# Operands of all projections at set distances in SBUF, with fewer places for staged copies

## The chip, the core and the metric

The kernel runs on one core of a Trainium2 chip. The core has a matrix engine (TensorE, PE in the profile, with its weight loads shown apart as PEld), a vector engine (DVE), a scalar engine (ACT), a general engine (POOL) and a sync engine (SP), which here only issues DMA transfers. All five run their own instruction streams and meet at semaphores. The metric is the device time of one execution in microseconds; the time before is 1488.55 us, the median of 3 runs (1488.12 to 1489.94).

## What is computed

One inference step of a one-layer streaming encoder: 1024 new frames (prompt) and 64 frames of a running stream (sample), 1088 tokens of 1024 features in all. Cut to what matters:

```python
def mixer(xn, conv_prefix, attn_fn, w_in, w_conv, w_conv_out, w_attn_out, w_out):
    proj = xn @ w_in
    cb, cc, ch, q, k, v, ga, gb = jnp.split(proj, splits, axis=-1)
    cv, conv_state = causal_conv(cc * ch, conv_prefix, w_conv)
    ya = (cb * cv) @ w_conv_out
    o, new_k, new_v = attn_fn(heads(q), heads(k), heads(v))
    yb = o.reshape(B, L, ATT_DIM) @ w_attn_out
    merged = jax.nn.sigmoid(ga) * ya + jax.nn.sigmoid(gb) * yb
    return merged @ w_out, conv_state, new_k, new_v

def swiglu(x, w1, w3, w2):
    return (jax.nn.silu(x @ w1) * (x @ w3)) @ w2

x = x + mixer(rmsnorm(x, g_mix), ...)
x = x + swiglu(rmsnorm(x, g_ffn), w_ff1, w_ff3, w_ff2)
return rmsnorm(x, g_final), ...
```

attn_fn is attention over the own chunk of 64 frames and the 8 before it, and q, k, v are 512 wide, ga and gb 1024, the inner size of swiglu is 2816. All is float32; the new key, value and convolution states are returned too.

## The kernel before

A float32 product is made of three products of a reduced type (F32R): `split` (L126, L127) writes the high part of an operand and the rest, called l = 0 and l = 1 for x and `hi` and `lo` (tags `wh`, `wl`) for weights, and hi times l0, hi times l1 and lo times l0 are summed in PSUM. The matrices of the input projection and of both parts of swiglu are moreover multiplied in halves with seven products of sums of blocks in place of eight (`STEPS`); the sums of x's blocks are tiles of their own (xs, tt), made once, and xn and mg are the plain blocks. All projections have features on the output's partitions and tokens in the columns: HT = 544 is half of the tokens, HN = 272 a quarter, and a matmul with 272 columns takes one quarter.

L246 in `run` is the inner statement of the seven-product projections: for each of four k it issues three matmuls (`hi` l0, `hi` l1, `lo` l0) on each of two quarters. Its x lies in [128, 2, 4, 544] tiles, that is l, then k, then the tokens, so that the two parts of one k are four rows apart; its weights lie in [128, 4, 128] tiles, a step of k after the other. L308 to L310 in `product` are the three terms of a plain product on quarters (the gates ga and gb, and the output projections of convolution and attention, whose operands u and ob are [128, 2, 4, 1088]). L487 to L489 in the v projection and L1101 to L1103 in w_out's projection have tokens on the partitions and 512 columns of weights moving. L1579 is the down projection of swiglu, which reads the inner values back from HBM (`ht`) as weights and 512 columns of w_ff2 from the rings `ring`; L1421 is the same for the 64 sample frames.

The stages in time, read from the trace by line: v projection and norm to 66 us, input units (q, k, cc, ch, cb, part of gb) to 328, gates with the attention between them to 560, merge to 678, w_out to 782, up projections of swiglu to 1252, then the down projection. Copies are staged on the way: `scr` is one region of SBUF in which `slot` hands out places by turns (`SNAP` for copies of partial sums out of PSUM, `CC` for the products cc, ch and k, `V32` for v rows on their way to the returned cache, `STAGE`, `UT` and so on), and a writer of a place waits until its last reader, often a DMA, is done. `st_pool` holds the gates on their way to HBM (`gst`), from which `gates_in` reads them back in the merge. Generators in the text (`ahead`, `prep`) mix the making of the next unit's weights into the running one, and that sets the order on the computing engines. On SP the order of the loads follows their destinations too: a load stands behind the work that frees its tile, and may stand far ahead of the place where the text asks for it. SP stops at a load whose destination is not yet free, and with it all loads behind. The first load of w2r (`early`, tag raw) is such a one.

## Time and profile before

| | |
|---|---|
| median of 3 runs | 1488.55 us |
| profiled execution | 1488.62 us |
| its span | 1486.9 us |
| mean granted clock of TensorE | 0.999 |
| stage of the up projections, busy time of PE in 462.00 us | 460.28 us, 3643 matmuls |
| stage of the down projection, in 235.00 us | 226.33 us, 1008 matmuls |
| input units, in 262.00 us | 261.44 us, 2080 matmuls |

The span is the time from the first to the last instruction in the profile; the execution's time lies 1.7 us above it. A matmul's busy time in the trace is that of one instruction from start to modelled end, and neighbours overlap; the interval between the starts of neighbours is what adds up to the stage. In the chain of waits a row like "PE Db L246 x24" gives when a group of 24 such matmuls began and how long it took until the next.

### The profile page before, as it was taken

To read this page: it belongs to the slowest core of one execution; us is meant where nothing else is said; L and a number is where in the kernel's file an instruction comes from. 1 tells how busy PE (TensorE), PEld (TensorE's weight loads), DVE (VectorE), ACT (ScalarE), POOL (GpSimd) and SP (SyncE) were. 2 spreads that over 40 slices of the span, in tenths; PEclk is the share of its full clock that TensorE was granted. 3 is DMA by queue.
4 is the path that set the end of the run, shared out by engine and by line. 5 is a ranking of instruction groups with operands and counts; after the bars stand their busy time and mean duration, and the time that the engine had idled before them with its cause. 6 is when DMAs were issued, how large, how long until landed. Compare 5 with 4: busy or idle time off the path is not lost.

```text
span 1486.9 us, 26478 instructions
## 1 busy us (share of the span) xinstructions
PE 1471.3 (99%) x10200; PEld 1380.9 (93%) x10200; DVE 982.5 (66%) x1852; ACT 681.7 (46%) x1398; POOL 129.9 (9%) x238
## 2 busy tenths in 40 slices
PE   9999999999999999999999999999999999999997
PEld 6899999999989999998889999999999999888886
DVE  7975565633777754763489667666666668857676
ACT  7654333434776653631356444444444445412223
POOL 1300010001111121000100111110011111000000
PEclk9999999999999999999999999999999999999999
DMA  8686623177776539645432454443344438767675
GB/s 290 183 275 209 202 66 113 58 219 222 191 190 180 146 109 297 194 122 174 150 106 79 146 184 156 160 146 117 114 146 154 152 149 306 262 227 238 224 265 202
DMA packets 166494, 264.73 MB, mean 178 GB/s; under 512 B 18912, under 2 KB 103072, under 8 KB 166208
## 3 DMA queue, kind: packets, MB, share of 16 engines
q1 hardware_dynamic: 145584, 196.13, 42.4%
q0 software_dynamic: 19632, 64.81, 12.1%
q10 hardware_dynamic: 1152, 2.10, 0.4%
q8 instruction: 80, 1.31, 0.4%
q14 instruction: 46, 0.38, 0.1%
HBM read 172.89 MB, written 91.92 MB: 178 GB/s over the span
## 4 chain that ended last, share of the span: by engine, by line
PE 95%; DVE 3%; DMA 1%; ACT 1%; issue 0%; SPq 0%; ACTq 0%; DVEq 0%
PE Ab L246 9%; PE Aa L246 9%; PE A L1579 8%; PE Db L246 4%; PE Da L246 4%; PE D L1579 4%; PE g L309 3%; PE g L308 3%; PE g L310 3%; PE Bb L246 2%; PE Ba L246 2%; PE B L1579 2%; PE wo L1102 2%; PE wo L1101 2%; PE wo L1103 2%; PE t L927 2%
## 5 line engine op out<-in xcount | busy, mean ns | idle before, releaser
L1579 PE MATMUL A<-ring,ht 128*128 128x512 f32 x528 | 124.3, 389 | 0.0
L1579 PEld LDWEIGHTS A<-ring,ht 128*128 128x128 f32 x528 | 98.9, 188 | 21.1 <-ACT acc L1589 0.6
L308 PE MATMUL g<-xn,whp 128*128 128x272 f32 x384 | 112.8, 294 | 0.0
L309 PE MATMUL g<-xn,whp 128*128 128x272 f32 x384 | 111.8, 291 | 0.0
L310 PE MATMUL g<-xn,wlp 128*128 128x272 f32 x384 | 111.1, 289 | 0.0
L126 ACT CAST ring<-w2r 128x512 fp32r<-128x512 f32 (+1 forms) x78 | 42.6, 587 | 89.5 <-PE A L1579 50.0
L126 ACT CAST hq<-sa 128x512 fp32r<-128x512 f32 x73 | 45.2, 619 | 80.5 <-DVE sa L1293 56.8
L838 DVE CUSTOM_DVE_ANT_0 p<-s,bb 128x640 f32<-128x640 f32 (+5 forms) x72 | 47.6, 662 | 42.4 <-PE s L881 40.6
L1277 POOL DMA_DIRECT2D h_d<-hq x73 | 38.9, 533 | 406.8 <-DVE hq L127 217.4
L308 PEld LDWEIGHTS g<-xn,whp 128*128 128x128 f32 x384 | 72.3, 188 | 0.9
L310 PEld LDWEIGHTS g<-xn,wlp 128*128 128x128 f32 x384 | 72.3, 188 | 0.5
L309 PEld LDWEIGHTS g<-xn,whp 128*128 128x128 f32 x384 | 72.4, 189 | 0.3
L127 DVE TENSOR_TENSOR hq<-sa,hq 128x512 fp32r<-128x512 f32 x73 | 50.4, 690 | 28.5 <-ACT hq L126 28.3
L127 DVE TENSOR_TENSOR wla<-rawa,wha 128x512 fp32r<-128x512 f32 x56 | 38.4, 688 | 39.6 <-ACT wha L126 39.6
L1579 PE MATMUL D<-ring,ht 128*128 128x512 f32 x264 | 62.6, 389 | 0.0
L246 PE MATMUL Aa<-tt,wha 128*128 128x272 f32 x352 | 58.4, 288 | 0.8 <-ACT sa_Q L234 0.8
L1579 PEld LDWEIGHTS D<-ring,ht 128*128 128x128 f32 x264 | 49.6, 188 | 10.3
L246 PE MATMUL Aa<-mg,wha 128*128 128x272 f32 x352 | 58.4, 288 | 0.4 <-DVE sa L1258 0.4
L246 PE MATMUL Ab<-mg,whb 128*128 128x272 f32 x352 | 58.6, 288 | 0.0
L246 PE MATMUL Ab<-tt,whb 128*128 128x272 f32 x352 | 58.4, 288 | 0.0
L126 ACT CAST wha<-rawa 128x512 fp32r<-128x512 f32 x56 | 34.6, 620 | 51.3 <-PE Ab L246 35.0
L127 DVE TENSOR_TENSOR ring<-w2r,ring 128x512 fp32r<-128x512 f32 (+1 forms) x78 | 48.7, 646 | 11.4 <-ACT ring L126 11.3
(531 smaller groups left out, 4379.8 us busy)
## 6 DMA issues: line engine op xcount, KB each, us to landing
ht<-h_d SPq DMA_DIRECT2D x154, 256.0 KB, 3.5
h_d<-hq POOLq DMA_DIRECT2D x73, 512.0 KB, 3.5
w2r<-in_w_ff SPq DMA_DIRECT2D x11, 1024.0 KB, 5.8
rawa<-in_w_ff SPq DMA_DIRECT2D x11, 1024.0 KB, 5.7
rawb<-in_w_ff SPq DMA_DIRECT2D x11, 1024.0 KB, 5.4
qd<-q_d SPq DMA_DIRECT2D x32, 272.0 KB, 4.7
rawp<-in_w_in SPq DMA_DIRECT2D x6, 1024.0 KB, 6.3
u_d<-scr SPq DMA_DIRECT2D x8, 544.0 KB, 5.2
```

What stands on the lines that cost most here:

```text
L126: a = act.copy(hi, src)
L127: b = vec.tensor_tensor(lo, src, hi.bitcast(F32), op=ALU.subtract)
L246: newest[0] = mm(t[:, j, :HN], w[:, k, :], x[p][:, l, k, j * HN : (j + 1) * HN], start=p in (1, 2, 7) and k == 0 and n == 0, stop=k == 3 a ...
L308: mm(out, a, p, start=k == 0, stop=False)
L309: mm(out, a, q, start=False, stop=False)
L310: mm(out, b, p, start=False, stop=k == kt - 1)
L838: vec.tensor_tensor_reduce(out=s if len(ps.shape) == 2 else s.rearrange("p (a b) -> p a b", a=2), in0=ps, in1=bias if len(ps.shape) == 2 e ...
L927: nc.tensor.transpose(tp[:, i * P : (i + 1) * P], s[:, i * P : (i + 1) * P], ident)
L1101: mm(ps, x(k, 0), wh, start=f, stop=False)
L1102: mm(ps, x(k, 0), wl, start=False, stop=False)
L1277: stored[0] = nc.gpsimd.dma_start(h_d[p, c - 1], hq.rearrange("p i l t -> p (i l t)").bitcast(F32)).ins
L1579: mm(t, ht[k][:, j, x], w[:, l], start=p in (1, 2, 7) and k == 0 and n == 0, stop=k == len(ks) - 1 and n == 2, skip_group_check=p in (6, 5 ...
```

## The change

It alters where operands lie, and gives other things fewer places.

- x's tiles (xn, mg, xs, tt; `operand`) become [k][l][tokens], the two parts of one k side by side, with rows of ROW = 552 floats of which the first 8 are unused; a lead of 8 floats stands ahead of xs.
- Weights (`pair`) get a step of 144 floats from k to k instead of 128, the high part beginning 8 floats into its tile. Where weights move (`moving_pair`: v and w_out) the high part of k begins at (56 + 16k) mod 64 floats and the low part at 16k mod 64. w_conv_out's and w_attn_out's weights get offsets of their own (`shift`) at the old step.
- u and ob get 8 floats between their two parts. In `product` the first two of the three terms change places for xn's even quarters.
- Staged copies: SNAP 4 places (5 before), CC 2 (3), a list KF for k's halves, V32 1 (2), `st_pool` 4 (5); gb is read back in 8 loads of [128, 1088] instead of 32 of [128, 272]; hs is one tile of two halves; two of the sums in the frames' norm lie in a `two_sums` tile of `early`; an accumulator moves from `dp` to `hp`; two of the four groups of cache transposes (`cache_tile`) come one step later.

```diff
 LAST = 3
+ROW, STEP = HT + 8, 144
 WARM = (14, 8)
...
         h = o // HT
-        return self.t[k // 4, h][:, l, k % 4, o - h * HT : o - h * HT + n]
+        return self.t[k // 4, h][:, k % 4, l, o - h * HT : o - h * HT + n]
...
+    def operand(pool, p, nm):
+        t = pool.tile([P, 8 * ROW], F32R, tag=f"o{p}", name=nm)
+        return t.rearrange("p (k l n) -> p k l n", k=4, l=2)[:, :, :, 8:]
+
+    def slots(nm):
+        return [ws.tile([P, 4 * STEP], F32R, tag=t, name=t + nm) for t in ("wh", "wl")]
+
+    def pair(nm):
+        hi, lo = (t.rearrange("p (k n) -> p k n", k=4) for t in slots(nm))
+        return hi[:, :, 8 : 8 + P], lo[:, :, :P]
+
+    def moved(nm, a, b):
+        hi, lo = slots(nm)
+        return hi[:, a : a + 512], lo[:, b : b + 512]
+
+    def moving_pair(nm, k):
+        return moved(nm, (56 + 16 * k) % 64, 16 * k % 64)
+
     def quarters(nm):
         return Quarters(
-            {gh: apool.tile([P, 2, 4, HT], F32R, tag=f"o{p}", name=f"{nm}{gh[0]}{gh[1]}") for p, gh in PLAIN.items()}
+            {gh: operand(apool, p, f"{nm}{gh[0]}{gh[1]}") for p, gh in PLAIN.items()}
         )
 
     def three_sums(pool, nm):
-        return {p: pool.tile([P, 2, 4, HT], F32R, tag=f"o{p}", name=f"{nm}{p}") for p in (6, 7, 5)}
+        return {p: operand(pool, p, f"{nm}{p}") for p in (6, 7, 5)}
 
     def both(t, c, n, src):
-        return split(t[:, 0, :, c : c + n], t[:, 1, :, c : c + n], src)
+        return split(t[:, :, 0, c : c + n], t[:, :, 1, c : c + n], src)
...
         def plain(self, p, src):
-            self.w[p] = [
-                ws.tile([P, 4, P], F32R, tag=t, name=f"{t}{self.nm}_{p}") for t in ("wh", "wl")
-            ]
+            self.w[p] = pair(f"{self.nm}_{p}")
             self.cast = split(*self.w[p], src)[0]
...
                         newest[0] = mm(
-                            t[:, j, :HN], w[:, k, :], x[p][:, l, k, j * HN : (j + 1) * HN],
+                            t[:, j, :HN], w[:, k, :], x[p][:, k, l, j * HN : (j + 1) * HN],
                             start=p in (1, 2, 7) and k == 0 and n == 0,
...
             for k in range(0, kt, 4):
-                hi, lo = (ws.tile([P, 4, P], F32R, tag=t, name=f"{t}p{prep.n}_{k}") for t in ("wh", "wl"))
+                nm = f"p{prep.n}_{k}"
+                if "shift" in ld:
+                    hi, lo = (t.rearrange("p (k n) -> p k n", k=4) for t in moved(nm, *ld["shift"]))
+                else:
+                    hi, lo = pair(nm)
                 split(hi, lo, ld["raw"][:, k : k + 4, at : at + P])
...
             p, q = x.at(0, k, o, n), x.at(1, k, o, n)
-            mm(out, a, p, start=k == 0, stop=False)
-            mm(out, a, q, start=False, stop=False)
+            first, then = (q, p) if x is xn and o // HN % 2 == 0 else (p, q)
+            mm(out, a, first, start=k == 0, stop=False)
+            mm(out, a, then, start=False, stop=False)
             mm(out, b, p, start=False, stop=k == kt - 1)
...
     for m in range(0, 8, 2):
-        lds = [{"src": ins[nm][0][:, m * P : (m + 2) * P], "w": 2 * P} for nm in ("w_conv_out", "w_attn_out")]
+        lds = [
+            {"src": ins[nm][0][:, m * P : (m + 2) * P], "w": 2 * P, "shift": shift}
+            for nm, shift in (("w_conv_out", (56, 24)), ("w_attn_out", (8, 40)))
+        ]
         plan += [(ld, 4, j * P) for ld in lds for j in range(2)]
...
     t1_pool = t1_stack.enter_context(tc.tile_pool(name="t1_pool", bufs=1, reuse_waits="tile"))
+    t1_pool.tile([P, 8], F32, name="lead1")
     t1 = three_sums(t1_pool, "xs")
 
-    scr = t1_pool.tile([P, 11496], F32, name="scr")
-    X, GM, SUMS, KEPT, VST, SQ, FEW = (0, 1024, 9312), 2048, 3072, (4096, 5120), (6144, 7168), 8192, 9264
-    V32 = [10336, 10848]
-    SNAP, STAGE, CC, UT = [544 * i for i in range(5)], [2720, 3808, 9312], [4896, 5988, 10400], [7080, 8172]
-    turn = {tuple(CC): 1}
+    scr = t1_pool.tile([P, 10816], F32, name="scr")
+    X, GM, SUMS, KEPT, VST, SQ, FEW = (0, 1024, 9264), 2048, 3072, (4096, 5120), (6144, 7168), 8192, 9216
+    V32 = [10288]
+    SNAP, STAGE, CC, UT = [544 * i for i in range(4)], [2720, 3808, 9264], [4896, 5988], [7080, 8172]
+    KF = [*CC, 2176]
+    turn = {tuple(KF): 0}
...
         for k in range(4):
-            hi, lo = (ws.tile([P, 512], F32R, tag=t, name=f"{t}v{half}_{k}") for t in ("wh", "wl"))
+            hi, lo = moving_pair(f"v{half}_{k}", k)
             if behind is None:
...
             x21_d[:, :, c : c + n],
-            xn.t[0, 1][:, :, :, c : c + n].rearrange("p l k t -> p (l k) t").bitcast(F32),
+            xn.t[0, 1][:, :, :, c : c + n].rearrange("p k l t -> p (k l) t").bitcast(F32),
         )
...
         def f(r, h, src, snap):
-            kf = slot(CC, HT)
+            kf = slot(KF, HT)
             whole(kf, src, snap)
...
         for _ in r:
-            if n < 2 and si in (2, 5):
+            if n < 2 and si in (2 + n, 5 + n):
                 i = 2 * n + si // 5
...
     pmm = pg_stack.enter_context(tc.tile_pool(name="pmm", bufs=3, space=PSUM, reuse_waits="tile"))
-    st_pool = pg_stack.enter_context(tc.tile_pool(name="st_pool", bufs=5, reuse_waits="tile"))
+    st_pool = pg_stack.enter_context(tc.tile_pool(name="st_pool", bufs=4, reuse_waits="tile"))
     att_stack = ExitStack()
...
     def gates_in(nm, m):
+        if nm == "gb":
+            t = mp.tile([P, T], F32, tag="rc", name=f"gb{m}", bufs=3)
+            nc.sync.dma_start(t, gb_d[m * P : (m + 1) * P])
+            for o, n in PIECES:
+                sg[nm, m, o] = t[:, o : o + n]
+            return
         for o, n in PIECES:
-            t = sg[nm, m, o] = mp.tile([P, HN], F32, tag=nm, name=f"{nm}{m}_{o}", bufs=8 if nm == "ga" else 4)
-            nc.sync.dma_start(t, (ga_d if nm == "ga" else gb_d)[m * P : (m + 1) * P, o : o + n])
+            t = sg[nm, m, o] = mp.tile([P, HN], F32, tag=nm, name=f"{nm}{m}_{o}", bufs=8)
+            nc.sync.dma_start(t, ga_d[m * P : (m + 1) * P, o : o + n])
 
     head_load(0)
 
-    nc.sync.dma_start(xn.t[0, 1].rearrange("p l k t -> p (l k) t").bitcast(F32), x21_d)
+    nc.sync.dma_start(xn.t[0, 1].rearrange("p k l t -> p (k l) t").bitcast(F32), x21_d)
     for i in range(4):
...
             uo = pg_stack.enter_context(tc.tile_pool(name="uo", bufs=1, reuse_waits="tile"))
-            u = Acts(uo.tile([P, 2, 4, T], F32R, name="u"))
-            ob = Acts(uo.tile([P, 2, 4, T], F32R, name="ob"))
+            u, ob = (
+                Acts(
+                    uo.tile([P, 2, 4 * T + 8], F32R, name=nm)[:, :, : 4 * T].rearrange("p l (k t) -> p l k t", k=4)
+                )
+                for nm in ("u", "ob")
+            )
             mp = pg_stack.enter_context(tc.tile_pool(name="mgp", bufs=4, reuse_waits="tile"))
...
             for k in range(4):
-                hi = ws.tile([P, 512], F32R, tag="wh", name=f"woh{hf}_{kq}_{k}")
-                lo = ws.tile([P, 512], F32R, tag="wl", name=f"wol{hf}_{kq}_{k}")
+                hi, lo = moving_pair(f"o{hf}_{kq}_{k}", k)
                 split(hi, lo, raw[:, k])
...
+        two_sums = early.tile([P, 2, D], F32, tag="raw", name="two_sums")
         w = wo_half(0)
...
             f = left.pop(c)
-            tag = "x1" if c == 384 else "sums"
-            s = wp.tile([P, D], F32, tag=tag, name=f"sums{c}", bufs=2 if c == 384 else 1)
+            if c == 384:
+                s = wp.tile([P, D], F32, tag="x1", name="sums384")
+            else:
+                s = two_sums[:, ORDER.index(8 if c == 512 else c // P + 4) // 2 % 2]
             s = s.rearrange("p (a k t) -> p a k t", a=2, k=4)[:, :, :, :n]
...
     LATE = {7: 1, 5: 2, 6: 6, 3: 7}
-    stored, last_keep, kept_now = [None], [], []
+    stored, last_keep, kept_now, both_hs = [None], [], [], {}
     names = [(l, p) for p in range(NF // 2) for l in "ab"]
...
                 return
-            hs = hp.tile([P, 2, 2, TS], F32R, tag="hs", name=f"hs{p}")
+            if "hs" not in both_hs:
+                both_hs["hs"] = hp.tile([P, 2, 256], F32R, tag="hs", name="hs", bufs=1)
+            hs = both_hs["hs"][:, p % 2].rearrange("p (r l t) -> p r l t", r=2, l=2)
             a, b, c, d = g[0, 0], g[0, 1], g[1, 0], g[1, 1]
...
             pool = apool if p in (1, 2, 4, 3) else tpool
-            ring[p] = pool.tile([P, 8 * HT], F32R, tag=f"o{p}", name=f"ring{p}")
+            ring[p] = pool.tile([P, 8 * ROW], F32R, tag=f"o{p}", name=f"ring{p}")[:, : 8 * HT]
         return ring[p]
...
         for kp in ks:
-            t = ws.tile([P, 2, 2, P], F32R, tag=("wh", "wl")[loaded[0] % 2], name=f"ht{kp}_{g}_{p}")
+            t = ws.tile([P, 4 * STEP], F32R, tag=("wh", "wl")[loaded[0] % 2], name=f"ht{kp}_{g}_{p}")
+            t = t[:, :512].rearrange("p (i l t) -> p i l t", i=2, l=2)
             loaded[0] += 1
...
     order = [(i + 4 * h, d) for g in range(2) for h, d in ((0, 0), (1, 0), (1, 1), (0, 1)) for i in (2 * g, 2 * g + 1)]
-    homes = [(dp, "acc")] + [(hp, "snap")] * 3 + [(hp, "sa"), (hp0, "snap"), (hp0, "sa")] + [(hp, "sa")] * 3
-    bufs = {(dp, "acc"): 1, (hp, "snap"): 3, (hp, "sa"): 4, (hp0, "snap"): 1, (hp0, "sa"): 1}
+    homes = [(hp, "snap")] * 3 + [(hp0, "snap"), (hp0, "sa")] + [(hp, "sa")] * 4 + [(hp, "hs")]
+    bufs = {(hp, "hs"): 1, (hp, "snap"): 3, (hp, "sa"): 4, (hp0, "snap"): 1, (hp0, "sa"): 1}
     for n, (i, d) in enumerate(order):```

Where the order of instructions moves. On TensorE, in the second unit of q (`Aq` and `Dq` are its sums in PSUM, xs and xn the moving x, `whq` and `wlq` its weights of step 6, 7 and so on; `ckp` are transposes of the key cache), before:

```order
L246 MATMUL Aq_788<-xs_103,whq_6_912 128x272 x4
L246 MATMUL Aq_788<-xs_103,wlq_6_913 128x272 x2
L701 MATMUL ckp_1094<-ident,scr 128x128 x4
L246 MATMUL Dq_1117<-xs_104,whq_7_943 128x272 x4
L246 MATMUL Dq_1117<-xs_104,wlq_7_944 128x272 x2
```

and in the changed kernel:

```order
L263 MATMUL Dq_1106<-xs_105,whq_7_944 128x272 x4
L263 MATMUL Dq_1106<-xs_105,wlq_7_945 128x272 x2
L728 MATMUL ckp_1135<-ident,scr 128x128 x4
L263 MATMUL Aq_789<-xs_106,whq_5_977 128x272 x4
L263 MATMUL Aq_789<-xs_106,wlq_5_978 128x272 x2
```

The third group of cache transposes stands behind step 7 instead of step 6, the fourth likewise one step later; nothing else on TensorE changes its place, and each k still issues four matmuls on the high part and two on the low one.

On SP, at the end of the merge (`gb` and `ga` are the gates read back, `w2r` a part of w_ff2, `xr` and `x_` residual rows, `wor` parts of w_out), before:

```order
L989 DMA gb_0_8161<-gb_d 128x272
L989 DMA gb_272_8163<-gb_d 128x272
L989 DMA gb_544_8165<-gb_d 128x272
L989 DMA gb_816_8167<-gb_d 128x272
L1361 DMA w2r_14218<-in_w_ff 128x2x1024
L1130 DMA gb_row<-in_g_ffn 128x1024
L1137 DMA xr_8311<-in_x_sample 64x512
```

and in the changed kernel, first at that place and then where the w2r load has gone:

```order
L1016 DMA gb_8120<-gb_d 128x1088
L1022 DMA ga_816_7902<-ga_d 128x272
L1022 DMA ga_0_7970<-ga_d 128x272
L1022 DMA ga_272_7972<-ga_d 128x272
L1022 DMA ga_544_7974<-ga_d 128x272
L1119 DMA wor_0_8521<-in_w_out 128x4x512
L1022 DMA ga_816_7976<-ga_d 128x272
L1119 DMA wor_1_8539<-in_w_out 128x4x512
L1166 DMA gb_row<-in_g_ffn 128x1024
```

```order
L1186 DMA x_7_8992<-in_x_prompt 128x512
L1187 DMA x_7_8992<-x_d 128x512
L1403 DMA w2r_14159<-in_w_ff 128x2x1024
L203 DMA rawa_9396<-in_w_ff 128x8x256
L203 DMA rawb_9598<-in_w_ff 128x8x256
```

The last gate tile of gb is asked for ahead of the last two of ga, in one load instead of four; the first w2r load has moved from ahead of `gb_row` to behind the last residual rows, ahead of the second unit's rawa and rawb.

## The prediction

> **What bounds the kernel now.** I read the first part of the page first, then the shares of the chain that ended last, then the longest waits of TensorE.
>
> ```profile
> span 1486.9 us, 26478 instructions
> PE 1471.3 (99%) x10200; PEld 1380.9 (93%) x10200; DVE 982.5 (66%) x1852; ACT 681.7 (46%) x1398; POOL 129.9 (9%) x238
> PE 95%; DVE 3%; DMA 1%; ACT 1%; issue 0%; SPq 0%; ACTq 0%; DVEq 0%
> PE warm L416 <- ACT ones L414: 2.9, 1, 2.9
> PE Aa L246 <- ACT sa_Q L234: 0.8, 1, 0.8
> PE Aq L246 <- DVE scr L560: 0.5, 1, 0.5
> ```
>
> TensorE is busy for 99% of the span, the chain lies on it for 95%, and of its waits the third longest is 0.5 us. No other engine is above 66%. The time is therefore the number of matmuls times the interval from one to the next; a change pays only if it changes one of the two. Each matmul has one weight load (10200 of each), and the loads are busy for 93%, so nearly every matmul streams while the next one's weights are being loaded.
>
> Next I looked at where the matmuls are, by source line, and what one costs. The columns of the first five rows are the stretch and its length, busy time of TensorE and of its weight loads with counts, the granted clock, DMA share and GB/s; the lines are, in this order, L246, L308, L1579, L1101 and L487.
>
> ```profile
> 0.00:1487.00 1487.00, 720.69 (x5712) 716.42 (x5712) 1.00 0.55 178
> 0.00:1487.00 1487.00, 186.38 (x640) 120.47 (x640) 1.00 0.55 178
> 0.00:1487.00 1487.00, 211.81 (x924) 173.23 (x924) 1.00 0.55 178
> 0.00:1487.00 1487.00, 50.85 (x128) 24.05 (x128) 1.00 0.55 178
> 0.00:1487.00 1487.00, 29.00 (x72) 13.11 (x72) 1.00 0.55 178
> 813.04 3.01 PE Db L246 x24
> 816.05 3.01 PE Ab L246 x24
> 843.11 3.01 PE Aa L246 x24
> 1307.24 4.08 PE D L1579 x18
> 1311.32 4.08 PE A L1579 x18
> 701.14 0.39 PE L1101 MATMUL wo<-woh,mg 128*128 128x512 f32 x1
> 706.70 0.39 PE L1101 MATMUL wo<-woh,mg 128*128 128x512 f32 x1
> ```
>
> L246 alone is half of the kernel: 5712 matmuls of 272 columns. From 813.04 to 843.11 the chain has ten such steps of 24, so 30.07 / 240 = 125.3 ns each. L308 to L310 are the three terms of one product, 3 x 640 = 1920 matmuls of 272 columns. The down projection, L1579, has 512 columns: 4.08 / 18 = 226.7 ns, 0.443 ns a column. L1101 to L1103 have 512 columns too, and between the two rows shown lie 24 matmuls: 5.56 / 24 = 231.7 ns. So the granted clock is 1.00 everywhere and still a column costs 0.443 ns in one line, 0.452 in another and 125.3 / 272 = 0.461 in a third. At the down projection's rate, 272 columns would take 120.4 ns. The difference can't be a wait for data: none stands there.
>
> What differs between these lines is where the operands lie. In L1579 the moving operand and the weights advance by whole multiples of 256 bytes, so that their distance, taken modulo 256 bytes, never changes. In L1101 each step of k moves only one of the two by a half of 256. In the up projections a row of x is 544 x 4 = 2176 bytes, 128 more than a multiple of 256, so that the distance alternates between two values from k to k. I tested that place matters at all on one product, in which nothing changes between its four pieces but the place of x, by 272 x 4 = 1088 bytes, that is 64 modulo 256:
>
> ```profile
> 597.22 0.29 PE L308 MATMUL yb<-ob,whp 128*128 128x272 f32 x1
> 598.73 0.29 PE L308 MATMUL yb<-ob,whp 128*128 128x272 f32 x1
> 600.23 0.29 PE L308 MATMUL yb<-ob,whp 128*128 128x272 f32 x1
> 601.71 0.29 PE L308 MATMUL yb<-ob,whp 128*128 128x272 f32 x1
> 603.22 0.29 PE L308 MATMUL ya<-u,whp 128*128 128x272 f32 x1
> ```
>
> Twelve matmuls lie between two rows: 1.51, 1.50, 1.48 and 1.51 us, or 125.8, 125.0, 123.3 and 125.8 ns each. Place is worth up to 2.5 ns in 125 here, and the four distances (moving operand to the weights that are loaded meanwhile) are 224, 160, 96 and 32 modulo 256. The third, 96, is the cheap one.
>
> **The change, part by part.** No matmul is added or removed, so every gain has to come from the interval.
>
> *Up projections, L246.* Rows of x become 2208 bytes with the two parts of one k side by side, weights of a step 576 bytes. From k to k x advances by 4416 and the weights by 576, both 64 modulo 256; the six matmuls of a k-step (three, for two halves) now show the same six distances in every k. Within one, x stands at 0, 64 (second half), 160, 224 (second part) and again 0, 64, modulo 256; the weights loaded meanwhile are those of the matmul that follows, high, high, high, low (32 lower), low and the next k's high (64 higher). With high and x starting level, as the tiles' sizes give, the distances are 0, 192, 96, 0, 224, 0. Before, even and odd k differed by 128. The trace has two rows for what a constant distance gives: 123.3 ns for the best piece, and the down projection's rate, 120.4. Against it stands that of the six new distances only one is 96, and that 224 was a dear piece. From above the bound is thus the dearest piece, 125.8 ns, a loss of 0.5. I take the best piece, 2.0 ns less, since that is the nearest row with 272 columns, and its k-steps are alike as those of the new layout are: 5712 x 2.0 = 11.4 us gained (ends: 28.0 gained, 2.9 lost).
>
> *Products, L308 to L310.* u and ob get a part that is 32 bytes further, xn the rows above, and the order of the two high terms is swapped for half the pieces of xn. u and ob had constant distances within a piece already, so only the mix changes there (three fifths of the matmuls, 1152, are gates on xn, in which k alternated). Mean of the four pieces above: (603.22 - 597.22) / 48 = 125.0 ns. With the same best piece, 1920 x 1.7 = 3.3 us gained (ends: 1920 x 4.6 = 8.8 gained, 1920 x 0.8 = 1.5 lost).
>
> *512 columns with moving weights* (L487 to L489 and L1101 to L1103, 3 x 72 + 3 x 128 = 600). Each k's place is shifted by 64 bytes so that the distance stays the same through k. Against the down projection they stand 5.0 ns higher; I take half of it, 600 x 2.5 = 1.5 us gained (ends: 3.0 gained, nothing). L1579 itself and the frames' line L1421 keep their distances: no term.
>
> *Fewer places for staged copies.* What each waits for, by its landing time:
>
> ```profile
> out_cache_v_prompt<-scr POOLq DMA_DIRECT2D x4, 256.0 KB, 4.1
> L498 POOL DMA_DIRECT2D out_cache_v_prompt<-scr x4: 552/564/569, 41.1 to 72.1; - x4
> ga_d<-gst POOLq DMA_DIRECT2D x32, 136.0 KB, 3.2
> gb_d<-gst POOLq DMA_DIRECT2D x16, 136.0 KB, 5.7
> gb<-gb_d SPq DMA_DIRECT2D x32, 136.0 KB, 2.4
> w2r<-in_w_ff SPq DMA_DIRECT2D x11, 1024.0 KB, 5.8
> 671.00 0.39 SPq L1361 DMA_DIRECT2D w2r<-in_w_ff  x1
> 804.81 0.38 SPq L184 DMA_DIRECT2D rawa<-in_w_ff  x1
> 811.54 0.62 ACT L126 CAST wha<-rawa 128x512 fp32r<-128x512 f32 x1 [2.39 <-DMA rawa<-in_w_ff]
> 825.07 3.01 PE Aa L246 x24
> ```
>
> The V staging keeps one place of two: the next copy must wait 4.1 us for the store, and the four stores start between 41.1 and 72.1 us, three gaps of some 10 us each, which cover it. The gates' staging has four places instead of five; one gate piece takes 24 matmuls, 24 x 125.0 = 3.0 us, so four cover 12 us against a landing of 5.7. The gb loads become 8 of four times the size, issued at least as far ahead as now; their issue costs SP less. One w2r load no longer goes out at 671.00 but behind the residual's loads, ahead of the weights at 804.81. Queued behind it on SP is that rawa load, and who waits for rawa is ScalarE's cast at 811.54: later by 5.8 us at most if the two share the bandwidth, against 825.07 - 811.54 = 13.5 us until TensorE starts on unit a. It is covered by 7.7 us. The casts write rows of 128 in place of 512, same elements, on engines with 34% and more to spare. Two of the cache's transposes come a step later, in the q units: same work. I put 1.5 us on all of it for a place or two that is missed, three times the longest wait of that kind shown above (0.5); ends 0 and 4 (one store awaited in full). If the cover of w2r were gone too, 5.8 us would stand on the path.
>
> *Sum.* -11.4 - 3.3 - 1.5 + 1.5 = -14.7 us. The profiled execution took 1488.6 us, 1.7 more than its span, and the median of the runs is 1488.55; I leave the 1.7 as it is: 1488.6 - 14.7 = 1474.
>
> The Trainium skill, TensorE: Matmul & The Clock Gate, section "Wait — 56ns, not 53.3ns?", gives a warm interval of N / 2.4 GHz plus about 2.5 ns, which would be 115.8 ns for 272 columns and 215.8 for 512. No row here shows that; the fastest 512-column row is 226.7 ns. An estimate by that page would be about 1407 us, if all lines came to it; my sum doesn't use it.
>
> **The rivals.**
>
> *All the way down.* If a distance that holds still lets the reads of matmul and weight load fall into step, as L1579's rows without spread may say, all lines reach 0.443 ns a column: -28.0 - 8.8 - 3.0 + 1.5, so 1450 us. For it: both steps of L1579 take exactly 4.08. Against it: the pieces of u and ob hold their distance through a piece already and run at 123.3 to 125.8.
>
> *Nothing.* Place averages out over six distances as it did over the old ones, with the same mean of 125 ns, or the interval has another cause (for one, the 272 columns themselves). Then only the 1.5 us of staging is left: 1490. For it: the mean of the four pieces above (125.0) is that of the steps of L246 (125.3), although their distances run differently. Against it: the four pieces themselves. A rule of the Trainium skill speaks for this case: SBUF — State Buffer, section "Who interferes with whom", has TensorE read moving operands and weights through two independent ports with no contention. By that rule the layout would be worth nothing; the pieces of 1.48 and 1.51 us disagree as far as they go.
>
> *Slower.* The six distances include 0 three times, and 192 and 224, and if these are at the dear end, the interval settles at or above the dearest piece. At 0.5 ns more on L246 and 0.8 on the products that is 2.9 + 1.5 = 4.4 us, with the staging 5.9, so 1494.5. It decides as soon as the mean of 24 matmuls in L246 is above 3.01 us; if constancy locks matmul and load into the bad phase, it may be more. For it: 224 was 125.8 above, and 96 comes up only once in six. Against it: L1579's distance is 0 in all of its matmuls and it has the best rate of all.
>
> **How the numbers follow.** Forecast (1474) 0.40, with a range of its own of 1466 to 1482, half or one and a half times its gain; all the way down (1450) 0.22; nothing (1490) 0.15; slower (1494.5 and above) 0.23. A measurement of this kernel tells about 0.2%, 3 us, from no change. Faster by more than that: the first two, 0.62, and 0.01 of the third. Within it: most of the third, 0.13. Slower: the fourth and a rest, 0.24. The range reaches from just under the second case to just above the fourth: 1448 to 1497.
>
> **What would show it.** The x24 rows of L246 on the chain would read 2.96 us in place of 3.01 (2.89 in the first rival, 3.01 in the second, 3.02 or more in the third). The pieces of yb and ya would still differ by place, with other times. 24 matmuls of L1101 would take about 5.50 us instead of 5.56. L1579's 18 stay at 4.08: if they move, the place is not the whole cause. The count stays 10200 and no wait of TensorE should be above 1 us but the first; a wait on V's staging, on st's places or on rawa near 812 would show the staging term wrong. The forecast fails if steps of L246 are unmoved or if they fall by more than 3%.

## The result, and the profile after

The changed kernel takes 1492.30 us (median of 12 runs, 1490.93 to 1494.96) against 1488.34 for the kernel before (12 runs): a ratio of 1.0026 with a 95% interval of 1.0017 to 1.0035. It is slower by 4 us, where 14.7 us less were forecast. The profiled execution took 1494.2 us, 1.9 above that median.

The first part of the page after, the shares of its chain, three of TensorE's waits, those at the merge (total, times and longest, in us), and two DMA pieces that stand on the chain (start, length, what):

```profile
span 1492.3 us, 26460 instructions
PE 1474.8 (99%) x10200; PEld 1384.6 (93%) x10200; DVE 981.5 (66%) x1852; ACT 680.4 (46%) x1398; POOL 129.9 (9%) x238
PE 89%; DMA 5%; DVE 3%; ACT 1%; SPq 1%; issue 1%; DVEq 0%; ACTq 0%
PE yb L331 <- DVE ob L128: 0.9, 1, 0.9
PE ya L330 <- DVE ga L1083: 0.8, 1, 0.8
PE yb L330 <- ACT ob L127: 0.5, 1, 0.5
555.31 19.27 DMA ob<-o_d
574.60 14.42 DMA rc<-rc_d
```

The count is 10200 as before and TensorE is still the bound, now busy for 3.5 us more. New on the chain are DMA pieces from 555 us on: ob's rows and their factors land late, and TensorE loses 3.0 us at the start of the merge, none in the kernel before. Whether that belongs to the change is asked below.

What one matmul costs shows in the same views as before: the totals of L263 (the old L246) by line, steps of 24 of it on the chain, the down projection, and two rows of w_out's line that lie 24 matmuls apart.

```profile
0.00:1493.00 1493.00, 724.48 (x5712) 720.15 (x5712) 1.00 0.55 177
902.08 3.02 PE Db L263 x24
905.10 3.02 PE Ab L263 x24
938.32 3.02 PE Bb L263 x24
1339.61 4.08 PE A L1621 x18
700.90 0.39 PE L1137 MATMUL wo<-who,mg 128*128 128x512 f32 x1
706.36 0.39 PE L1137 MATMUL wo<-who,mg 128*128 128x512 f32 x1
```

A step of 24 went from 3.007 to 3.02 us: 36.24 us for the twelve steps from 902.08 to 938.32, 125.8 ns a matmul, where 125.2 to 125.3 stood. That alone is 724.48 - 720.69 = 3.8 us over the kernel, nearly the 4.0 us that the median lost. The 512-column line of w_out did fall, 5.46 us for 24 where 5.56 stood, and the down projection did not move. So the agreement of 3.8 and 4.0 is not the whole account: a gain of some 1.3 us in w_out and the lost time at the merge stand beside it, with opposite signs.

### The profile page after: what moved, and what is told of

Read it like the earlier page. It is cut to its first block, busy times and chain, and to the rows that moved or that the text cites. A ratio compares the mean times of both kernels' runs of the same rounds, so it can differ in the third digit from the quotient of the medians.

```text
span 1492.3 us, 26460 instructions
## 1 busy us (share of the span) xinstructions
PE 1474.8 (99%) x10200; PEld 1384.6 (93%) x10200; DVE 981.5 (66%) x1852; ACT 680.4 (46%) x1398; POOL 129.9 (9%) x238
## 4 chain that ended last, share of the span: by engine, by line
PE 89%; DMA 5%; DVE 3%; ACT 1%; SPq 1%; issue 1%; DVEq 0%; ACTq 0%
PE Ab L263 9%; PE Aa L263 9%; PE A L1621 8%; PE Db L263 4%; PE Da L263 4%; PE D L1621 4%; PE Bb L263 2%; PE Ba L263 2%; PE B L1621 2%; PE wo L1138 2%; PE wo L1137 2%; PE wo L1139 2%; PE t L954 2%; PE Ak L263 2%; PE Acb L263 2%; PE Ach L263 2%
## 5 line engine op out<-in xcount | busy, mean ns | idle before, releaser
L1621 PE MATMUL A<-ring,ht 128*128 128x512 f32 x528 | 124.0, 389 | 0.0
L1621 PEld LDWEIGHTS A<-ring,ht 128*128 128x128 f32 x528 | 99.1, 188 | 20.6
L330 PE MATMUL g<-xn,whp 128*128 128x272 f32 x384 | 113.1, 294 | 0.0
L331 PE MATMUL g<-xn,whp 128*128 128x272 f32 x384 | 111.7, 291 | 0.0
L332 PE MATMUL g<-xn,wlp 128*128 128x272 f32 x384 | 110.7, 288 | 0.0
L127 ACT CAST ring<-w2r 128x512 fp32r<-128x512 f32 (+1 forms) x78 | 42.6, 587 | 89.0 <-PE A L1621 50.3
L127 ACT CAST hq<-sa 128x512 fp32r<-128x512 f32 x73 | 45.2, 619 | 81.1 <-DVE sa L1332 55.8
L330 PEld LDWEIGHTS g<-xn,whp 128*128 128x128 f32 x384 | 72.3, 188 | 1.0
L332 PEld LDWEIGHTS g<-xn,wlp 128*128 128x128 f32 x384 | 72.4, 189 | 0.5
L331 PEld LDWEIGHTS g<-xn,whp 128*128 128x128 f32 x384 | 72.4, 188 | 0.3
L128 DVE TENSOR_TENSOR hq<-sa,hq 128x512 fp32r<-128x512 f32 x73 | 50.3, 690 | 30.1 <-ACT hq L127 29.9
L128 DVE TENSOR_TENSOR wla<-rawa,wha 128x512 fp32r<-128x512 f32 x56 | 38.4, 688 | 40.1 <-ACT wha L127 40.1
L1621 PE MATMUL D<-ring,ht 128*128 128x512 f32 x264 | 62.6, 389 | 0.0
L263 PE MATMUL Aa<-tt,wha 128*128 128x272 f32 x352 | 58.6, 288 | 0.8 <-ACT sa_Q L251 0.8
L1621 PEld LDWEIGHTS D<-ring,ht 128*128 128x128 f32 x264 | 49.6, 188 | 10.3
L263 PE MATMUL Aa<-mg,wha 128*128 128x272 f32 x352 | 58.6, 288 | 0.4 <-DVE sa L1297 0.4
L263 PE MATMUL Ab<-mg,whb 128*128 128x272 f32 x352 | 58.8, 288 | 0.0
L263 PE MATMUL Ab<-tt,whb 128*128 128x272 f32 x352 | 58.6, 288 | 0.0
L127 ACT CAST wha<-rawa 128x512 fp32r<-128x512 f32 x56 | 34.6, 620 | 52.0 <-PE Ab L263 35.5
L128 DVE TENSOR_TENSOR ring<-w2r,ring 128x512 fp32r<-128x512 f32 (+1 forms) x78 | 48.6, 645 | 11.5 <-ACT ring L127 11.5
```

The lines of the kernel that those rows point to most:

```text
L127: a = act.copy(hi, src)
L128: b = vec.tensor_tensor(lo, src, hi.bitcast(F32), op=ALU.subtract)
L263: newest[0] = mm(t[:, j, :HN], w[:, k, :], x[p][:, k, l, j * HN : (j + 1) * HN], start=p in (1, 2, 7) and k == 0 and n == 0, stop=k == 3 a ...
L330: mm(out, a, first, start=k == 0, stop=False)
L331: mm(out, a, then, start=False, stop=False)
L332: mm(out, b, p, start=False, stop=k == kt - 1)
```

## The experiments

Intervals below are differences of neighbouring starts in the trace, averaged over a line without the places where TensorE waited. "Distance" is always that from the moving operand to the weights loaded meanwhile, modulo 256 bytes; it is worked out from the sizes and offsets of the tiles, since the trace holds no addresses. What speaks for the working out is that on u, ob and mg the same pattern of intervals comes back where it puts the same distance. All of these kernels are built on the changed one and keep its fewer places for copies. One of these still moves u and ob: the place that `st_pool` gave up is 1088 bytes, 64 modulo 256, so that with the old weights their four quarters stand at 32, 224, 160 and 96 instead of 224, 160, 96 and 32. The four values are the same, the cheap one comes a quarter later, and where the expectations below list such quarters, the list is to be read shifted by one.

**1. Old distances, fewer places.** Everything that was put in to set a distance is undone (the cut shows three of the places).

```diff
-ROW, STEP = HT + 8, 144
+ROW, STEP = HT, 128
...
-        return t.rearrange("p (k l n) -> p k l n", k=4, l=2)[:, :, :, 8:]
+        return t.rearrange("p (l k n) -> p l k n", l=2, k=4)
...
-        return moved(nm, (56 + 16 * k) % 64, 16 * k % 64)
+        return moved(nm, 0, 0)
```

> The changed kernel with every operand back at its old distance (x as l, k, tokens in rows of 2176 bytes, weights at a step of 512, u and ob without the 32 bytes, no shifts of moving weights, no swapped terms); the fewer places for staged copies stay. Theory A (the loss is the place of the operands): the interval in the seven-product line goes back from 125.8 to 125.2 ns, 5712 x 0.66 = 3.7 us less, the 512-column lines of w_out go back from 228.5 to 232 ns, 1.3 us more, and the total is some 2 us under the changed kernel. Theory B (the loss is the staging): total as in the changed kernel, the waits of the merge near 590 us stay, and the intervals don't matter.

Measured: 1490.03 us, ratio to the kernel before 1.0003 (0.9994 to 1.0013); the seven-product line at 125.1 to 125.2 ns, as before, w_out's line back at 232 ns. The chain shows it at once:

```profile
900.32 3.01 PE Ab L263 x24
903.33 3.01 PE Db L263 x24
939.41 3.01 PE Db L263 x24
```

So theory A holds: the loss lies in the operands' places. The staging, in all its edits together, costs no more than the interval of this comparison, 0.13% or 2 us, and perhaps nothing.

**2 to 4. The same constancy at other distances.** A pad moves all weight tiles down against x.

```diff
+    pad = ctx.enter_context(tc.tile_pool(name="pad", bufs=1, reuse_waits="tile", side="right"))
+    pad.tile([P, 40], F32, name="pad")
     ws = ctx.enter_context(tc.tile_pool(name="ws", bufs=8, reuse_waits="tile", side="right"))
```

(40, 24 and 48 floats.)

> The changed kernel with a pad of 160 bytes that moves all weight tiles down against x: still the same six distances in every k, but 96, 32, 192, 96, 64, 96 instead of 0, 192, 96, 0, 224, 0; the down projection stands at 96 in place of 0. Theory V (each distance has its price, as the pieces of the old kernel show: 0 126.3, 32 125.3, 64 124.2, 96 123.5, 192 126.2, 224 126.1 ns): mean 124.4 against 125.8, 5712 x 1.4 = 8 us less, total near 1484, and the down projection falls by up to 2.8 ns of its 226.7. Theory C (only that the distance is constant counts): all intervals stay, total near 1492.

> As before with a pad of 96 bytes: distances 160, 96, 0, 160, 128, 160, down projection at 160. Theory V (with 128 at 125.5 and 160 at 125.2): mean 125.2, 3.7 us less than the changed kernel, down projection 1 ns less. Theory C: no change.

> As before with a pad of 192 bytes: distances 64, 0, 160, 64, 32, 64, down projection at 64. Theory V: mean 124.9, 5 us less than the changed kernel, down projection 2 ns less. Theory C: no change.

Measured: 1498.2, 1499.4 and 1500.3 us. The seven-product line stands at 125.46, 125.45 and 125.80 ns. Theory V asked for 124.4, 125.2 and 124.9; theory C for 125.81 three times. Both fall: the value makes less than it should, and not in the order that it should, and the down projection, which theory V had falling by up to 2.8 ns, became slower. What made these kernels 6 to 8 us slower than the changed one is the down projection, whose own distance the pad shifted from 0 to 96, 160 and 64. A step of 18 of it on the chain of the first of them:

```profile
1338.32 4.22 PE A L1623 x18
1342.53 4.22 PE D L1623 x18
```

4.08 became 4.22: 234.4 ns in place of 226.7, and 233.3 in the other two. Only the place of the weights had changed there. That is some 7.6 ns for 512 columns, 7 us over its 924 matmuls; place is worth more there than anything the change touched, and before and after it stood at the best of the four.

**5 and 6. The distance held from matmul to matmul.** The quarter becomes the outer loop, k runs 0, 2, 1, 3, and odd weights lie 128 bytes further, so that ten of the twelve matmuls of a quarter stand at one distance; the sixth and the twelfth don't.

```diff
-            for k in range(4):
-                for n, (w, l) in enumerate(((hi, 0), (hi, 1), (lo, 0))):
-                    for j in range(2):
+            for j in range(2):
+                for k in (0, 2, 1, 3):
+                    for n, (w, l) in enumerate(((hi, 0), (hi, 1), (lo, 0))):
...
```

> The first of these kernels (old distances, fewer places for copies) with the distance held from matmul to matmul, not only from k to k: in the seven-product line the quarter is the outer loop, k runs 0, 2, 1, 3, and the weights of odd k lie 128 bytes further, so that a step stands at one distance for 12 matmuls but one: 0 and then 192 (on xs 32 and then 224). w_out's weights the same, k evens then odds, at 0 throughout as the down projection. The output projections of the mixers stand at 0, 192, 128, 64 in their four pieces in place of 224, 160, 96, 32. Theory H (a distance that is held sets the rate, 0 is best, as in the down projection: 226.7 ns at 0 and 233.3 to 234.2 at 64, 96 and 160): w_out falls from 232 to 226.7, half of the seven-product line (at 0) to 120.4 or at most 123, the line to 123.5 or less, 9 us less. Theory F (a matmul of 272 columns pays a fixed part that place hardly moves on the mean): the line stays at 125.2 within 0.7, total 1488 to 1492.

> The same at other distances: the seven-product line at 128 and then 64 (on xs 160 and then 96), w_out held at 192. Theory H: w_out at 233 or so, as the down projection where it stands away from 0; the seven-product line at its own price for each of the four, at least 1 ns apart from each other as the pieces 224, 160, 96, 32 are (126.1, 125.4, 123.4, 125.3). Theory F: the line within 0.7 of 125.2.

Measured: 1494.4 and 1492.8 us. w_out's line fell to 227.7 to 228.8 ns at distance 0 (226.7 was asked for), 228.3 to 231.1 at 192. The seven-product line did not fall: 126.06 and 125.54 ns. Theory H is wrong for 272 columns, and u and ob show it in one row after another. These are the first matmuls of five successive pieces of yb in the first of the two kernels, from a second quarter on, at distances 0, 192, 128, 64 and again 0:

```profile
596.05 0.29 PE L332 MATMUL yb<-ob,whp 128*128 128x272 f32 x1
597.55 0.29 PE L332 MATMUL yb<-ob,whp 128*128 128x272 f32 x1
599.07 0.29 PE L332 MATMUL yb<-ob,whp 128*128 128x272 f32 x1
600.58 0.28 PE L332 MATMUL yb<-ob,whp 128*128 128x272 f32 x1
602.06 0.28 PE L332 MATMUL yb<-ob,whp 128*128 128x272 f32 x1
```

1.50, 1.52, 1.51 and 1.48 us. Over all pieces the price of a held distance on u and ob, with the kernel before for the odd multiples of 32, is 125.7 at 0, 125.3 at 32, 123.5 at 64, 123.5 at 96, 126.2 at 128, 125.1 at 160, 126.3 at 192, 126.1 at 224: a mean of 125.2 with a spread of 2.8. (The list in the expectation of kernel 7 has up to 0.4 more.) And 0, best for 512 columns, is an ordinary one here: 125.7 ns, not 120.4.

**7 to 9. Held at 96 and 32; ob's loads first; the changed kernel again.** The weights of the held kernel go 96 bytes further, gates included; in the second kernel ob's and its factors' loads are issued ahead of u's.

```diff
-                t.rearrange("p (b n) -> p b n", b=2)[:, :, 0 : 0 + 256].rearrange("p b (a n) -> p b a n", a=2)
+                t.rearrange("p (b n) -> p b n", b=2)[:, :, 24 : 24 + 256].rearrange("p b (a n) -> p b a n", a=2)
...
```

> The loop order of the held kernels (quarter outside, k in the order 0, 2, 1, 3, odd weights 128 bytes further), for the gates too, with the weights 96 bytes further: the seven-product line and the gates stand at 96 for the first quarter and at 32 for the second; w_out is held at 0; u and ob at their old distances 224, 160, 96, 32. The prices of held distances, read from the pieces of the old kernel and of the first held one, are 0 125.8, 32 125.4, 64 123.9, 96 123.4, 128 126.5, 160 125.5, 192 126.3, 224 126.0 ns. Theory P (these prices hold wherever the distance is held): the line (123.4 + 125.4) / 2 = 124.4, 4.3 us under the kernel before, gates 1.3 us less, w_out 1.5 us less, in all some 7 us, 1481.5. Theory F (the mean doesn't move): the line at 125.2 or above, total 1487 or above.

> The same, with the loads of ob and its factors issued ahead of those of u. If TensorE's waits at the start of the merge (3 us in the profiled run of the changed kernel) come from ob's loads being late behind u's 4.4 MB, they go, and the products' gaps fall by 1 to 3 us; u then lands later, and if it is late the wait turns up at ya in their place and nothing is gained.

> The changed kernel once more, unaltered, for a second profile of it. If the 3 us that TensorE lost at the start of the merge belong to the change, they stand there again; if they were one execution's luck, the span is 1489 to 1490 and the waits on ob are under 1 us in all. The intervals by line stay as they were to 0.05 ns.

Measured: 1494.0 us for the first, the line at 125.83 ns; theory P falls. 1497.8 for the second: the wait moved to ya, which stood 3.5 us for u's loads, so that order is worse. The changed kernel again: 1493.2 us, ratio 1.0041 (1.0024 to 1.0059), so slower by 4 us once more; its intervals of the seven-product line, the products and the down projection the same to 0.1 ns, and no wait on ob among the ten longest. The span was 1491.3, where 1489 to 1490 was asked for if the 3 us at the merge were one execution's luck. The full 3 us were that execution's; that the change has no part in them is not shown. TensorE lost 1.0 to 1.8 us at the same place in kernels 5, 6, 7, 10, 13 and 14, 0.2 to 0.4 in 1, 2, 4 and in this one, and nothing in 3, 11 and 12. What decides it no run tells. The margin is thin: in the kernel before, ob's last part was ready at 591.7 us, and the first matmul that reads it started at 592.5; any delay of those loads beyond 0.8 us goes to the path.

**10 and 11. All operands moved together; w_out alone.** Same distances as in kernel 7, x and weights 96 bytes elsewhere; and kernel 1 with w_out's part of the held kernels only.

```diff
+    apad = ctx.enter_context(tc.tile_pool(name="apad", bufs=1, reuse_waits="tile", side="right"))
+    apad.tile([P, 24], F32, name="apad")
     apool = ctx.enter_context(tc.tile_pool(name="apool", bufs=1, reuse_waits="tile", side="right"))
```

> The kernel held at 96 and 32 with all operands (x, weights, rings) moved together by 96 bytes: every distance is as there, but x stands at 128 and 192 modulo 256 and the weights at 224, as in the pieces of u and ob that took 123.4 and 125.4 ns. Theory D (the distance alone sets the interval): the seven-product line stays at 125.8 (125.4 at distance 96, 126.4 at 32). Theory XW (place of x and place of the weights both count): 123.4 at 96 and 125.4 at 32, up to 0.5 more for the two of twelve that lie at another distance, the line at 124.8, 6 us under that kernel. Theory R (neither; what differs is the stage, with other engines' and DMA traffic): as theory D in this line, while u and ob keep 123.4 to 126.

> The kernel with the old distances everywhere and the fewer places for copies, and of the held kernels only w_out's part: its moving weights held at distance 0 (odd k 128 bytes further, k evens then odds). If the gain in that line belongs to it alone: 231.9 to 228.3 ns over 384 matmuls, 1.4 us less there, all other lines as with the old distances (seven-product line 125.15), total 1.4 us under it, 1487 to 1488.5: no more than the measurement can tell from the kernel before.

Measured: the seven-product line of the first at 125.84 ns, group by group as in kernel 7 (125.5 in quarters at 96, 126.2 in those at 32), the total 1492.6: only distances count, not places by themselves, theory D as far as it goes. On u and ob the cheap piece moved with the distance: 64 came at another quarter and took 123.5. The second came to 1489.2 us, ratio 1.0004 (0.9995 to 1.0013), with w_out's line at 227.9 to 229.2 ns: the gain is real in its line and too small to be told in the total.

The traces show where the 125.5 in mg's quarter at 96 and the 123.5 in ob's part come from. The intervals of a group of twelve, in ns, as medians over its repetitions, on ob in kernel 7 (above) and on mg in the first of these (below), where the sixth and the twelfth matmul meet weights of the next k at 224:

```
ob, 96:  128 121 126 121 126 121 126 121 126 121 126 121
mg, 96:  128 121 126 121 126 124 126 124 127 125 135 123
```

They agree for five matmuls. Then one foreign distance comes, and of the six matmuls behind it five stand at 96 again and don't find back. At that point x and the weights have also both moved by 128 bytes, and this trace can't tell the one from the other.

**12. No foreign distance.** The terms of a k run low part first, and the low parts lie where the loads need them.

```diff
-                    for n, (w, l) in enumerate(((hi, 0), (hi, 1), (lo, 0))):
+                    for n, (w, l) in enumerate(((lo, 0), (hi, 0), (hi, 1))):
...
+            for t, o in zip(slots(nm), (0, 32))
```

> The kernel held at 96 and 32, now without the one foreign distance that stood in every six matmuls there: the terms of a k run low part first, and low parts lie where the weights that are loaded during the matmul before have to lie, so that all twelve matmuls of a quarter stand at 96, then all twelve of the next at 32, k in its plain order. Gates likewise. Weights moved by a pad; down projection and w_out kept at 0, u and ob at 224, 160, 96, 32. In the held kernels the first five intervals of a quarter at 96 were 128, 121, 126, 121, 126 ns, as in ob's piece that took 123.4, and after the foreign distance they became 126, 124, 127, 125, 135. Theory L (matmul and weight load fall into a pattern that lasts until a foreign distance breaks it): 123.4 at 96 and 125.4 at 32, the line at 124.4 in place of 125.8, 4.3 us under the kernel before, gates 1.3 and w_out 1.4 us less: some 1482. Theory N (the seven-product line has another reason for its 125.2 to 125.8, such as the traffic of its stage): the line stays at 125.4 or above and the total at 1489 or above.

Measured: 1497.1 us, the line at 126.35 ns, the worst of all. Theory L as I had put it is wrong, and theory N, another cause in the stage, came as it was put; the next two experiments decide about it. The low weights now stood 128 bytes off the high ones, so that the distance to the weights in use changed from matmul to matmul, though that to the weights being loaded did not.

**13 and 14. Nothing moves modulo 256.** Rows of xn and mg are made 2304 bytes, nine times 256, the quarter is the outer loop; xs and tt keep 2176 for comparison. In the second kernel the weights stand 64 bytes elsewhere, so that 96 follows 160.

```diff
...
+        w = WIDE if pool is apool else HT
+        t = pool.tile([P, 8 * w], F32R, tag=f"o{p}", name=nm)
+        return t.rearrange("p (l k n) -> p l k n", l=2, k=4)[:, :, :, :HT]
```

(WIDE = 576.)

> The kernel with the old distances, with two edits in the seven-product line: the quarter outside, and rows of xn and mg 2304 bytes long (a multiple of 256) so that x and weights both keep their place from matmul to matmul, as u and ob do: both the weights in use and those being loaded stand at 96 for all twelve matmuls of a quarter and at 32 for the next twelve. xs and tt keep rows of 2176 bytes and serve for comparison (their 0/128 and 192/64 alternate with k). Gates on xn follow. w_out and v stand at 160 through, down projection at 0, u and ob at 64, 0, 192, 128. Theory L2 (a place pays only where nothing moves modulo 256, neither x nor weights): on mg and xn 123.4 at 96 and 125.4 at 32, mean 124.4; on xs and tt 125 to 125.5; the line at 124.7, 2.3 us under the kernel before, gates 1.3 less. Theory N (another cause in the stage): mg like tt, 125.2 or above.

> The last kernel with the weights 64 bytes elsewhere: xn and mg stand at 160 for the first quarter and at 96 for the second, so that 96 follows 160 as it does in u's and ob's pieces, where its twelve intervals begin 128, 121, 126, 121 at once. In the last kernel 96 came at the start of a step and began 123, 126, 131, 125, 124, 125, 125, 124 before it fell into 126, 121, 126, 121. Theory M (the intervals depend on the state that the matmuls before left, and settle only after up to eight): 96 on mg takes 123.4 from its first matmul on, 160 up to 126 at its start, mean of both 124.6 in place of 125.1; the seven-product line 0.3 ns less, 1.5 us, on a total that can hardly be told from the last one. Theory K (the first matmuls of a step are slow whatever the distance, for a reason of the step): 96 stays at 125 or begins as 160 does.

Measured: 1490.5 and 1489.5 us (1.0006 and 1.0005 of the kernel before, both within 0.16% of it), the line at 125.22 and 124.87 ns. On mg the first gave 125.3 at 32, interval for interval the pattern of ob's piece at 32, and 124.6 to 124.8 at 96: eight irregular matmuls, then 126, 121, 126, 121. In the second, with 160 ahead, 96 ran 126, 121, 126, 121 on mg from the start on and took 123.4; 160 took 125.0, with the cycle of ob's piece at 160. On xn the same order of distances did less: 96 took six matmuls or more to fall into the cycle and came to 124.1. So theory M holds and K falls, and theory N with it: mg and tt share the stage and the loop, and only mg, whose rows keep their place, got there. Chain steps of 24 from the second kernel; the first two and the last are steps on tt, the four between are mg's:

```profile
901.03 3.01 PE Db L266 x24
904.03 3.01 PE Ab L266 x24
907.04 2.98 PE Db L266 x24
910.02 2.98 PE Ab L266 x24
913.00 2.98 PE Aa L266 x24
915.98 2.98 PE Ba L266 x24
918.96 3.01 PE Aa L266 x24
```

2.98 against 3.01: 1%, the most that place gave the 272-column line in any layout. No version was faster than the kernel before. Rows of 2304 bytes for xs and tt as well would at best take the line to the mean of 123.4 and 125.4; that is an estimate of 4.3 us under the kernel before, 5712 x (125.15 - 124.4). It needs 3 KB more in each partition and was not tried, and xn's 124.1 speaks for less.

## Why the prediction was wrong

**What bounds the kernel.** Right: 10200 matmuls, no other engine took their place, and up to 3 us of waits at the merge apart, the result is the sum of intervals.

**Up projections, -11.4 us.** This step failed. It read 123.3 ns off ob's best piece and gave it to the new layout because "its k-steps are alike as those of the new layout are". In ob's pieces the distance stays the same from each matmul to the next; in the new layout it runs through 0, 192, 96, 0, 224, 0 within a k and then repeats. Experiments 13 and 14 show that 123.4 is the state of a run in which nothing moves modulo 256, reached only after up to eight matmuls, and kernels 7 and 10 that it is lost again within a group, where one matmul meets a foreign distance and the operands move. In the new layout the distance changes at nearly every matmul, and the line took 125.81 where 125.15 stood, +3.8 us. The prediction's own row for a mixture was L246 before, whose distance alternates: it took about the mean of the four pieces, which the prediction cites under the rival called nothing. The measured loss lies past the 2.9 us that I had drawn from the dearest piece, but the line does not lie past that piece: the bound was read from single rows as 125.8 - 125.3 = 0.5 ns, and over all pieces the dearest took 126.1, the line 125.15. By the prices of held distances the new mixture (0 three times, 192, 96, 224) would take 125.5, but the same sum missed in kernels 2 to 4: what sets the interval of a mixture stays open.

**Products, -3.3 us.** The same step, with the same fault. The mean of the three lines stayed at 125.3 ns. Cheap and dear pieces changed hands.

**512 columns, -1.5 us.** w_out's part came as forecast and a little more: 5.46 us for 24 matmuls against the 5.50 that the prediction wrote, 3.4 ns over 384 matmuls, 1.3 us less. In v's line two terms fell a little and one stood (232.0, 231.2, 229.1 against 232.8, 231.2, 231.1): 0.2 us over 216 matmuls.

**Staging, +1.5 us.** 0.5 by experiment 1, with an interval from 0.9 gained to 1.9 lost. The cover that the prediction named for w2r, V and the gates' places held; none of them is among TensorE's longest waits. The wait that did come, on ob at the merge, is not among those that the prediction looked at.

**The rivals.** The one called slower is what came: its place, its sign, and within 2.2 us its time (1494.5). That closeness is in part luck: its price for L246 was 0.5 ns, measured 0.66, its 1.5 us for the products was not there, and it had neither w_out's gain nor the wait on ob. "All the way down" rested on time per column, 0.443 x 272 = 120.4 ns, and that quotient was no rate. Held at 0, 272 columns take 125.7 and 512 take 226.7: by the line through these two, 0.42 ns for each further column and 11 ns for each matmul whatever its width. Other widths in the profile before lie near that line, though in other stages and at other places: the median interval of 256 columns is 120 ns, of 288 132, of 320 147 and of 384 175.5, where it gives 119, 133, 146 and 173. The 120.4, which also stood as the far end of the gain, was reached at no distance that was held here. A reader can get this from the profile before: 226.7 and 125.3 differ by 101.4 for 240 columns, 0.42 again.

**The estimate of 1407 us.** By its own prices it leaves out the down projection: 924 x (226.7 - 215.8) is 10 us more, so that it should read 1397. The forecast doesn't use it.

**What would show it.** The x24 row was the right one to name, and 3.02 was the value given there for the rival that came. The 18 of the down projection stayed at 4.08 and the count at 10200, as written there.

## What to carry to other kernels

Before a rate is carried from one matmul to another of a different width, fit a fixed part and a part per column to two widths; a quotient mixes them. Before a price is carried from one place in the program to another, list what changes from one instruction to the next in both: "the same every k-step" gave 125.8 ns here, and "the same at every matmul" 123.4 at its best distance. And an edit of addresses moves everything that shares the pool: a pad of 160 bytes, put in for the seven-product line, cost the down projection 7 us.

## What the runs showed of the hardware

Where TensorE did not wait, with the granted clock at 1.00, the interval of a 272-column matmul ran from 119 to about 137 ns and that of 512 columns from 224 to 241. Means over a piece of u and ob at a held distance went from 123.5 to 126.3 ns by the relative place of moving operand and weights modulo 256 bytes. In the up projections the pattern repeats: in the profiles before, after, 7, 13 and 14, 98 of 100 intervals or more lie within 1 ns of the median of their place in the group; on xn and xs it repeats less well. The intervals have a memory: they fall into a cycle (126, 121 at 96; 130, 120, 125, 124, 127 at 160) after up to eight matmuls at one distance, and in kernels 7 and 10 they left it where one matmul stood at another and the operands moved. The mean of the seven-product line stayed between 124.9 and 126.4 ns in all of these kernels, so that place is a second-order matter there.

The Trainium skill, SBUF — State Buffer, section "Who interferes with whom", gives TensorE a port for moving operands and one for weights that don't disturb each other. The down projection at 4.08 and 4.22 us for 18, with only the weights' place changed, doesn't fit with full independence. Which part of the path the two share, no run here tells. The fixed part of 11 ns also differs from the 2.5 ns of the Trainium skill, TensorE: Matmul & The Clock Gate, section "Wait — 56ns, not 53.3ns?", which is measured there with bf16 matmuls where these are F32R; its slope of 1 / 2.4 GHz, 0.417 ns a column, agrees with the 0.42 measured.
